# A Griffin-style decoder block on one core: the recurrence by decay products on VectorE, the output gate moved to the first block, and the sums of a wide block taken together

## The chip, the core and the metric

The kernel runs on one core of a Trainium2 chip. A core has TensorE (matrix multiply, results in PSUM banks of 128 x 512 float32), VectorE, ScalarE and GpSimd (elementwise work), and SyncE, which here only issues DMA. Every engine takes its instructions in order and waits on semaphores. The metric is the device time of one execution in microseconds (us). Times of before: 1763.41, 1767.73 and 1767.49, median 1767.49.

## What is computed

One layer of a decoder block on x of 256 x 2048, all float32 (the reference, shortened):

```python
a = rmsnorm(h, norm_mix_pre)
proj = a @ w_in                       # 2048 x 17408
q_a, k_a, v_a, q_r, f_r, i_r, g_r, gate_a, gate_r = split_columns(proj)
attn = ...   # 3 groups of 8 heads, windows 128, 512, 2048 with strides 1, 4, 16, rotary
q_h = silu(q_r); f = lb + (1 - lb) * sigmoid(f_r)         # 8 heads, 128 keys, 128 values
r_out = hgrn2(q_h, log(f), 1 - f, i_r)    # S_t = diag(f_t) S_{t-1} + k_t v_t^T, o_t = S_t^T q_t
r_out = rmsnorm_per_head(r_out) * gain * silu(g_r)        # g_r: the output gate
y = sigmoid(gate_a) * (attn @ w_attn_branch) + sigmoid(gate_r) * (r_out @ w_hgrn_branch)
h = h + rmsnorm(y @ w_mix_out, norm_mix_post)
gt, up = split(rmsnorm(h, norm_ffn_pre) @ w_ffn_gate_up)  # 2 x 5632 columns
h = h + rmsnorm((silu(gt) * up) @ w_ffn_down, norm_ffn_post)
```

The recurrence over 256 positions can be written as o_t = sum over s <= t of (q_t . D(s,t) k_s) v_s, with D(s,t) the product of the decays f after s up to t, for each of 128 keys. So per head it is a 256 x 256 lower triangle of weights, times v.

## The kernel before

**Weights.** All weights come as float32 through three buffers `raw` on SyncE's queue. A split makes two parts for TensorE: ScalarE copies `raw` into a rounded high part (`w`, L294 or L340), VectorE subtracts to get the low part (L295, or `wl` in L342). A product is three matmuls: high x high, high x low, low x high (`prod`, L372). The activations are split the same way (`Split`, L459; `transpose_in`, L509, makes `xT` with a ScalarE copy in L524 and a VectorE subtraction in L528).

**Items.** The program is one list of items, written out by hand in the loop at L1444. For item i it issues the split of item i+2 (`AHEAD`), the loads as far as the `raw` buffers reach, the matmuls of item i, then one turn of the evacuations (`evacs`), and one turn of each of two *lanes*. A lane is a queue of Python generators (the recurrence of half the heads, the attention of one head); each turn issues a generator's instructions up to its next `yield`. So on every engine the lanes' instructions stand between those of the weights.

**Wide blocks.** The first eight blocks (`early`, L1379) and the FFN work on 1024 columns in eight steps of 256 rows (`Wide`, `split_wide` L331, `multiply_wide` L363). Plain steps take 24 matmuls. In three steps of each block but the first, seven products of sums replace eight (21 matmuls): `split_wide` builds sums of weight quarters on VectorE (L346 to L353) and splits them in two sets, `w`/`wl` (L358 the last of it) and `dh`/`dl` (L360, VectorE's last instruction of such a split). The products p1, p5, p6 and p7 have banks of their own; after the third such step (`last7`) `gather` (L417) copies p1 on ScalarE (L421) and adds the others on VectorE (L422 to L425) into four tiles `b.rest`. The four banks of the block are added to them at its end, in `totals` (L705, sums in L712) for the early blocks and in `evac_ffn` (L1249, L1252) for the FFN. `totals` takes bank after bank: add, then use; a `yield` after every second one.

In these steps `by_sums` goes first and `by_raw`, which ends p1, second (L411). Between the two, and between the halves of a plain step, `between` gives the block's `mid` and the lanes a turn.

The first block has no seven-product steps. It is also where x is transposed: its `mid` (`more_x`, L663) transposes the next two row blocks of x in the middle of step c. The split of item c+2 and its loads stand before that in the program (L1454).

The order of the early blocks is: two of attention gates, one of the recurrence's branch gate, three of values v (these six go through a sigmoid or copy on ScalarE, L726, and to DRAM on ScalarE's queue, L729), then the output gate `g` (`evac_g`, L741: a sigmoid on ScalarE, L747, and two VectorE operations, L748 and L751, per bank), then the recurrence's values `i`.

**Chunks.** The projections for f, q of the recurrence and q, k of the attention come transposed, in steps of 16 matmuls (`multiply_chunk`). Their evacuations include the rotary embedding on VectorE (L786 to L793).

**The recurrence** (`recurrence`, L853) runs twice, for four heads each, on tiles of 128 keys x 1024 (head, position). VectorE clamps f at 2^-63, ScalarE takes Ln, VectorE scans it into running sums b (L870). Then blocks of size w = 1, 2, 4, ..., 32 are joined level by level: GpSimd subtracts the sum at the middle of each pair of blocks (L878), ScalarE takes Exp of both halves (L881, L882), VectorE multiplies the left half by k (L884), GpSimd the right half by q (L885), TensorE takes eight small products, and VectorE puts them into the weights `at` where a mask says so (L896). Levels 64 and 128 (`level64`, `level128`) and the diagonal (`same`) are alike. The levels depend on b alone, so a new one starts every second turn and several are under way at once.

Of the kernel before, what the change touches and what calls it, by code (L numbers as in the profile page):

```python
# [31 lines left out]
F_MIN = 2.0 ** -63  # L32
# [49 lines left out]
def tile_hybrid_block(ctx: ExitStack, tc: tile.TileContext, t, out):  # L82
# [13 lines left out]
    def nm(s):  # L96
        serial[0] += 1
        return f"{s}_{serial[0]}"
# [7 lines left out]
    def aux():  # L106
        return auxp.tile([P, 512], F32, tag="aux", name=nm("aux"))
# [60 lines left out]
    reset = kp.tile([P, 1024], F32, name="reset")  # L168
    nc.gpsimd.memset(reset, 1.0)
    nc.gpsimd.memset(reset.rearrange("p (n w) -> p n w", w=64)[:, :, 0:1], 0.0)  # L170
# [10 lines left out]
    def fslot(s):  # L181
        return fp[0].tile([P, 1024], F32, tag="f", bufs=16, name=nm(s))
# [90 lines left out]

    def multiply(i):
        kind, n = items[i][:2]
        if kind is chunks:
            multiply_chunk(n)
            return
        b, c = steps[n][:2]

        def between():
            if b.mid:
                b.mid(c)
            advance_lanes()

        multiply_wide(n, between=between)
# [76 lines left out]
    def multiply_wide(n, sides=(0, 1), groups=(0, 1), between=lambda: None):  # L363
# [341 lines left out]
    def totals(b, then):  # L705

        while "r1c" not in ready:
            yield
        for n, key in enumerate(((0, 0), (0, 1), (1, 0), (1, 1))):
            src = b.bank[key]  # L710
            if b.rest:
                nc.vector.tensor_add(b.rest[key], src, b.rest[key])  # L712
                src = b.rest[key]
            then(key, src)
            if n % 2:
                yield
# [136 lines left out]
    def recurrence(half):  # L853
# [4 lines left out]
        def spans(x, w):  # L858
            return x.rearrange("p (n w) -> p n w", w=w)

        kk, b, at = fslot("kk"), fslot("b"), fslot("at")
# [8 lines left out]
        nc.vector.tensor_tensor_scan(  # L870
            out=b, data0=reset, data1=f, initial=0.0, op0=OP.mult, op1=OP.add,
        )
        yield
        def level(lev, w):
            x = fslot("x")
            xv, bv, kv, qv = (spans(a, 2 * w) for a in (x, b, kk, q))
            n = 1024 // (2 * w)
            nc.gpsimd.tensor_sub(xv, bv, bv[:, :, w - 1 : w].to_broadcast([P, n, 2 * w]))  # L878
            yield
            left, right = slice(0, w), slice(w, 2 * w)  # L880
            nc.scalar.activation(xv[:, :, left], xv[:, :, left], AF.Exp, scale=-1.0)  # L881
            nc.scalar.activation(xv[:, :, right], xv[:, :, right], AF.Exp)  # L882
            yield
            nc.vector.tensor_mul(xv[:, :, left], xv[:, :, left], kv[:, :, left])  # L884
            nc.gpsimd.tensor_mul(xv[:, :, right], xv[:, :, right], qv[:, :, right])  # L885
            yield
            yield
            ps = aux()
            for e in range(8):
                xe = x[:, e * P : (e + 1) * P]  # L890
                mm(
                    spans(ps[:, e * 64 : (e + 1) * 64], w), xe,
                    spans(xe, 2 * w)[:, :, right], True, True,
                )
            yield
            nc.vector.copy_predicated(  # L896
                at.rearrange("p (e n w) -> p e n w", e=8, w=2 * w)[:, :, :, right],
                lmask[:, lev, :].rearrange("p (n w) -> p n w", w=w)[:, None, :, :]
                .to_broadcast([P, 8, 64 // w, w]).bitcast(I32),
                ps.rearrange("p (e n w) -> p e n w", e=8, w=w),  # L900
            )

        def level64():

            x = fslot("x")
            xe, be, ke, qe = (
                a.rearrange("p (e c t) -> p e c t", e=8, c=2) for a in (x, b, kk, q)
            )
            nc.gpsimd.tensor_sub(
                xe[:, :, 0, :], be[:, :, 0, :], be[:, :, 0, 63:64].to_broadcast([P, 8, 64])  # L910
            )
            yield
            nc.scalar.activation(xe[:, :, 0, :], xe[:, :, 0, :], AF.Exp, scale=-1.0)
            nc.scalar.activation(xe[:, :, 1, :], be[:, :, 1, :], AF.Exp)
            yield
            nc.vector.tensor_mul(xe[:, :, 0, :], xe[:, :, 0, :], ke[:, :, 0, :])
            nc.gpsimd.tensor_mul(xe[:, :, 1, :], xe[:, :, 1, :], qe[:, :, 1, :])
            yield
            yield
            ps = aux()  # L920
            for e in range(8):
                mm(ps[:64, e * 64 : (e + 1) * 64], xe[:, e, 0, :], xe[:, e, 1, :], True, True)
            yield
            nc.scalar.activation(
                at.rearrange("p (e t) -> p e t", e=8)[:64, :, 64:],
                ps[:64].rearrange("p (e t) -> p e t", e=8), AF.Copy,
            )

        def level128():

            x = fslot("x")
            xc, bc = (a.rearrange("p (h c t) -> p h c t", h=4, c=4) for a in (x, b))
            end = small("end")
            nc.vector.tensor_add(end[:, :4], bc[:, :, 0, 63], bc[:, :, 1, 63])
            nc.vector.tensor_sub(
                xc[:, :, 0, :], bc[:, :, 0, :], end[:, :4, None].to_broadcast([P, 4, 64])
            )
            nc.gpsimd.tensor_sub(
                xc[:, :, 1, :], bc[:, :, 1, :], bc[:, :, 1, 63:64].to_broadcast([P, 4, 64])
            )  # L940
            nc.gpsimd.tensor_add(
                xc[:, :, 3, :], bc[:, :, 3, :], bc[:, :, 2, 63:64].to_broadcast([P, 4, 64])
            )
            yield
            xh, kh, qh = (a.rearrange("p (h t) -> p h t", h=4) for a in (x, kk, q))
            nc.scalar.activation(xh[:, :, :P], xh[:, :, :P], AF.Exp, scale=-1.0)
            nc.scalar.activation(xc[:, :, 2, :], bc[:, :, 2, :], AF.Exp)
            nc.scalar.activation(xc[:, :, 3, :], xc[:, :, 3, :], AF.Exp)
            yield
            nc.vector.tensor_mul(xh[:, :, :P], xh[:, :, :P], kh[:, :, :P])  # L950
            nc.gpsimd.tensor_mul(xh[:, :, P:], xh[:, :, P:], qh[:, :, P:])
            yield
            yield
            ps = aux()
            for h in range(4):
                mm(ps[:, h * P : (h + 1) * P], xh[:, h, :P], xh[:, h, P:], True, True)
            yield
            a2.append(ptile("a2"))
            nc.scalar.activation(a2[0], ps, AF.Copy)

        def same():

            x = fslot("x")
            nc.gpsimd.tensor_mul(x, q, kk)
            yield
            yield
            ps = aux()
            for e in range(8):
                mm(ps[:, e : e + 1], x[:, e * P : (e + 1) * P], ones[:, 0:1], True, True)
            yield  # L970
            nc.vector.copy_predicated(
                at.rearrange("p (e t) -> p e t", e=8),
                ident[:, None, :].to_broadcast([P, 8, P]).bitcast(I32),
                ps[:, :8, None].to_broadcast([P, 8, P]),
            )

        a2 = []
        todo = [level(lev, w) for lev, w in enumerate(LEVELS)] + [same(), level64(), level128()]
        running, turn = [], 0
        while todo or running:  # L980
            if turn % 2 == 0 and todo:
                running.append(todo.pop(0))
            for r in list(running):
                try:
                    next(r)
                except StopIteration:
                    running.remove(r)
            turn += 1
            yield
        a2 = a2[0]  # L990
# [384 lines left out]
    def begin_wides():  # L1375
# [3 lines left out]
    early = [  # L1379
        (("a", 0), ("a", 1), COL_GA, 512),  # L1380
# [4 lines left out]
    early += [("g", "g", COL_GR, 512), ("i", "i", COL_IR, 512)]  # L1385
# [58 lines left out]
    for i in range(len(items)):  # L1444
# [94 lines left out]
```

## Time and profile before

| | us |
|---|---|
| times of three runs | 1763.41, 1767.73, 1767.49 |
| the profiled execution: time | 1764.46 |
| the profiled execution: span from the first to the last instruction | 1762.7 |
| mean granted TensorE clock over the span | 0.994 |

A row of the profile's groups or time line names the line of the kernel, engine, operation, output <- inputs by the program's names (buffer numbers left out), the shapes, and how many. In a time line start and duration stand in front, and in brackets how long the engine was idle before it and which instruction ended that. In a list of waits the numbers are us in total, times, and the longest. A row of busy times by stretch has the stretch, its length, then busy us of PE (TensorE's matmuls), PEld (its weight loads), DVE (VectorE), ACT (ScalarE) and POOL (GpSimd), each with the number of instructions, then the granted TensorE clock, the share of DMA time and GB/s. Matmuls overlap each other, so a matmul's drawn duration is longer than the distance to the next.

### The profile page before, as it was taken

How to read it: one execution, taken by the hardware profiler on the slowest of the kernel's cores; microseconds unless marked ns; L12 is line 12 of the kernel's file. 1: busy time of each engine (PE TensorE's matmuls, PEld its weight loads, DVE VectorE, ACT ScalarE, POOL GpSimd, SP SyncE). 2: the span in 40 equal slices, each digit the busy share in tenths (PEclk: the TensorE clock that was granted, in tenths of full speed). 3: DMA queues.
4: the chain of work that ended last, by engine and by line, in shares of the span. 5: the costliest groups of instructions: out<-in, count | busy, mean ns of one | idle time of the engine just before them, and what ended most of it. 6: DMA issues, size and time to landing. Idle time of an engine off the chain costs nothing.

```text
span 1762.7 us, 21573 instructions
## 1 busy us (share of the span) xinstructions
PE 1719.0 (98%) x8356; PEld 1432.1 (81%) x8357; DVE 1390.0 (79%) x1466; ACT 917.3 (52%) x1052; POOL 77.2 (4%) x54
## 2 busy tenths in 40 slices
PE   8999999899999999999999999999999999999997
PEld 6777777688888888888888877888888888788886
DVE  5878888866798997775566477888888888899998
ACT  6555555444534544445444466555555555565663
POOL 0000000000151241000000000000000000000000
PEclk9999999999999999999999999999999999999999
DMA  7656666465535534466555755555555555666563
GB/s 266 225 200 223 223 221 221 152 203 186 185 120 167 201 122 158 154 203 236 170 160 175 264 166 192 200 198 197 192 191 191 191 191 191 215 215 210 189 200 118
DMA packets 207190, 338.49 MB, mean 192 GB/s; under 512 B 10688, under 2 KB 77424, under 8 KB 207088
## 3 DMA queue, kind: packets, MB, share of 16 engines
q1 hardware_dynamic: 201360, 325.71, 55.8%
q10 hardware_dynamic: 5728, 11.41, 1.7%
q8 instruction: 65, 1.06, 0.3%
q14 instruction: 37, 0.30, 0.1%
HBM read 328.69 MB, written 8.39 MB: 191 GB/s over the span
## 4 chain that ended last, share of the span: by engine, by line
PE 70%; DVE 16%; issue 6%; ACT 5%; DMA 2%; ACTq 0%; POOL 0%; SPq 0%; DVEq 0%; POOLq 0%
PE acc L119 47%; PE aux L119 21%; DMA raw<-in_w_in 2%; DVE wl L358 2%; DVE wl L342 2%; DVE dl L360 2%; DVE w L295 2%; ACT w L354 1%; DVE e L1252 1%; DVE sum L346 1%; ACT w L340 1%; DVE sum L353 1%; DVE sum L352 1%; ACT e L726 1%; DVE e L1258 1%
## 5 line engine op out<-in xcount | busy, mean ns | idle before, releaser
L295 DVE TENSOR_TENSOR w<-raw,w 128x1024 fp32r<-128x1024 f32 x224 | 284.9, 1274 | 173.7 <-ACT w L294 172.8
L119 PE MATMUL acc<-xT,w 128*128 128x256 f32 (+1 forms) x2048 | 369.6, 340 | 5.2 <-DVE w L295 5.2
L294 ACT ACTIVATE w<-raw 128x1024 fp32r<-128x1024 f32 x224 | 236.3, 1057 | 255.6 <-PE acc L119 236.9
L119 PEld LDWEIGHTS acc<-xT,w 128*128 128x128 f32 x2048 | 312.4, 189 | 51.3 <-DVE w L295 7.4
L342 DVE TENSOR_TENSOR wl<-raw,w 128x2048 fp32r<-128x2048 f32 (+1 forms) x131 | 283.9, 2173 | 64.5 <-ACT w L340 61.6
L340 ACT ACTIVATE w<-raw 128x2048 fp32r<-128x2048 f32 (+1 forms) x131 | 237.3, 1817 | 71.0 <-issue 22.3
L358 DVE TENSOR_TENSOR wl<-sum,w 128x2048 fp32r<-128x2048 f32 x63 | 144.4, 2291 | 59.0 <-ACT w L354 57.7
L119 PE MATMUL acc<-w,hT 128*128 128x512 f32 x622 | 184.8, 391 | 1.5 <-DVE w L295 1.2
L119 PE MATMUL acc<-w,xT 128*128 128x512 f32 x578 | 172.4, 396 | 5.7 <-ACT xT L524 3.8
L351 ACT ACTIVATE w<-sum 128x1024 fp32r<-128x1024 f32 x63 | 66.9, 1062 | 171.1 <-DVE sum L346 168.3
L119 PE MATMUL aux<-w,hT 128*128 128x512 f32 x430 | 138.0, 389 | 0.0
L119 PEld LDWEIGHTS acc<-w,hT 128*128 128x128 f32 x622 | 115.8, 188 | 27.0 <-DVE w L295 2.5
L119 PEld LDWEIGHTS acc<-w,xT 128*128 128x128 f32 x578 | 108.8, 190 | 29.7 <-ACT xT L524 4.2
L119 PE MATMUL aux<-w,xT 128*128 128x512 f32 x344 | 112.3, 395 | 1.6 <-ACT w L340 1.6
L360 DVE TENSOR_TENSOR dl<-raw,dh 128x1536 fp32r<-128x1536 f32 x63 | 110.3, 1752 | 0.0
L357 ACT ACTIVATE dh<-raw 128x1536 fp32r<-128x1536 f32 x63 | 93.2, 1480 | 4.7 <-PE aux L119 2.1
L119 PEld LDWEIGHTS aux<-w,hT 128*128 128x128 f32 x430 | 80.7, 188 | 16.7
L119 PE MATMUL acc<-w,yT 128*128 128x512 f32 x384 | 88.2, 390 | 0.0
L119 PE MATMUL acc<-w,a 128*128 128x512 f32 x268 | 83.8, 389 | 1.7 <-DVE e L1252 1.7
L119 PEld LDWEIGHTS acc<-w,yT 128*128 128x128 f32 x384 | 71.8, 188 | 15.2 <-DVE w L295 0.4
L119 PE MATMUL aux<-w,a 128*128 128x512 f32 x268 | 83.7, 389 | 0.0
L119 PE MATMUL aux<-wl,hT 128*128 128x512 f32 x215 | 83.6, 389 | 0.0
(278 smaller groups left out, 2742.9 us busy)
## 6 DMA issues: line engine op xcount, KB each, us to landing
raw<-in_w_in SPq DMA_DIRECT2D x270, 512.0 KB, 4.6
raw<-in_w_ffn_gate_up SPq DMA_DIRECT2D x176, 512.0 KB, 4.6
raw<-in_w_ffn_down SPq DMA_DIRECT2D x88, 512.0 KB, 4.8
raw<-in_w_mix_out SPq DMA_DIRECT2D x32, 512.0 KB, 4.9
raw<-in_w_hgrn_branch SPq DMA_DIRECT2D x16, 512.0 KB, 4.9
raw<-in_w_attn_branch SPq DMA_DIRECT2D x16, 512.0 KB, 4.7
waits<-e ACTq DMA_DIRECT2D x24, 256.0 KB, 4.6
v<-waits SPq DMA_DIRECT2D x6, 512.0 KB, 8.2
```

What stands on the lines that cost most here:

```text
L119: nc.tensor.matmul(ps, lhsT, rhs, start=start, stop=stop, skip_group_check=True)
L294: nc.scalar.activation(wh, raw, AF.Copy)
L295: nc.vector.tensor_sub(wl, raw, wh.bitcast(F32))
L340: nc.scalar.activation(hi[:, c], raw[:, c], AF.Copy)
L342: nc.vector.tensor_sub(lo[:, c], raw[:, c], hi[:, c].bitcast(F32))
L346: nc.vector.tensor_sub(s[:, :1024].rearrange("p (a c) -> p a c", a=2), raw[:, 512:1536].rearrange("p (a c) -> p a c", a=2), raw[:, None, : ...
L351: nc.scalar.activation(hi[:, :1024], s[:, :1024], AF.Copy)
L352: nc.vector.tensor_add(s[:, 1024:1536], raw[:, 512:1024], s[:, 512:1024])
L353: nc.vector.tensor_sub(s[:, 1536:], raw[:, 1536:], s[:, 1024:1536])
L357: nc.scalar.activation(dhi, d, AF.Copy)
L358: nc.vector.tensor_sub(lo, s, hi.bitcast(F32))
L360: nc.vector.tensor_sub(dlo, d, dhi.bitcast(F32))
```

## The change

Five edits, the diff cut to its core.

1. The first block is the output gate `g`; the others keep their order.
2. Where a wide block has a `mid` (only the first block), the split of item i+2 and its loads are issued in the middle of step i, behind the transposes, and no longer ahead of the step.
3. In the third seven-product step of a block (where the activations need no preparation) `by_raw` goes first, so that p1 is complete 12 matmuls before the step's end.
4. `totals` adds all four banks to `b.rest` in one go, and uses them in the next two turns.
5. The recurrence. No Ln, no scan, no Exp. k and q are kept multiplied by the decay products of their block, in place: after the products of a level are taken, the left halves of k are multiplied by the whole product of the right block, and the right halves of q by that of the left block; the block products (`end`) are multiplied in pairs. All of it is on VectorE; only the clearing of `at` stays on GpSimd. One level follows the other: products, one turn later the mask copy and three multiplies, two turns later the next products. The float32 pool gets 17 tiles instead of 16, in place of the tile `reset`.

```diff
@@ prepare, multiply
+    def prepare(i):
+        split(i + AHEAD)
+        if i + AHEAD < len(items):
+            load_upto(items[i + AHEAD][2] + N_RAW)
...
         def between():
             if b.mid:
                 b.mid(c)
+                prepare(i)
             advance_lanes()
@@ multiply_wide
-        for part in (by_raw, by_sums) if b.prep else (by_sums, by_raw):
-            part()
-            if part is by_raw or not b.prep:
-                between()
-                between = lambda: None
+        first, second = (by_raw, by_sums) if b.prep or last else (by_sums, by_raw)
+        first()
+        between()
+        second()
@@ totals
-        for n, key in enumerate(((0, 0), (0, 1), (1, 0), (1, 1))):
-            src = b.bank[key]
-            if b.rest:
-                nc.vector.tensor_add(b.rest[key], src, b.rest[key])
-                src = b.rest[key]
-            then(key, src)
-            if n % 2:
+        keys = ((0, 0), (0, 1), (1, 0), (1, 1))
+        if b.rest:
+            for key in keys:
+                nc.vector.tensor_add(b.rest[key], b.bank[key], b.rest[key])
+            yield
+        for key in keys:
+            then(key, b.rest[key] if b.rest else b.bank[key])
+            if key == (0, 1):
                 yield
@@ recurrence
-        nc.vector.tensor_scalar(f, f, F_MIN, None, op0=OP.max)
-        yield
-        nc.scalar.activation(f, f, AF.Ln)
-        yield
-        nc.vector.tensor_tensor_scan(
-            out=b, data0=reset, data1=f, initial=0.0, op0=OP.mult, op1=OP.add,
...
+        nc.vector.tensor_mul(x, q, kk)
+        yield
+        nc.vector.tensor_mul(q, q, f)
+        yield
+        ps = aux()
+        for e in range(8):
+            mm(ps[:, e : e + 1], x[:, e * P : (e + 1) * P], ones[:, 0:1], True, True)
+        yield
+        nc.vector.copy_predicated(
...
+        ends, used, end = fslot("end"), 0, f
+        for lev, w in enumerate(LEVELS):
             ps = aux()
             for e in range(8):
+                es = slice(e * P, (e + 1) * P)
                 mm(
+                    spans(ps[:, e * 64 : (e + 1) * 64], w), kk[:, es],
+                    spans(q[:, es], 2 * w)[:, :, w:], True, True,
                 )
             yield
             nc.vector.copy_predicated(
...
+            n = 1024 // (2 * w)
+            end = spans(end, 2)
+            for x, l, r in ((kk, slice(0, w), 1), (q, slice(w, 2 * w), 0)):
+                y = spans(x, 2 * w)[:, :, l]
+                nc.vector.tensor_mul(y, y, end[:, :, r : r + 1].to_broadcast([P, n, w]))
+            new = ends[:, used : used + n]
+            used += n
+            nc.vector.tensor_mul(new, end[:, :, 0], end[:, :, 1])
+            end = new
+            yield
+            yield
...
+        end = spans(end, 2)
+        for x, c in ((ke, 0), (qe, 1)):
+            nc.vector.tensor_mul(
+                x[:, :, c, :], x[:, :, c, :],
+                end[:, :, 1 - c : 2 - c].to_broadcast([P, 8, 64]),
+            )
...
@@ the early blocks and the loop
     early = [
+        ("g", "g", COL_GR, 512),
         (("a", 0), ("a", 1), COL_GA, 512),
...
-    early += [("g", "g", COL_GR, 512), ("i", "i", COL_IR, 512)]
+    early += [("i", "i", COL_IR, 512)]
...
-        split(i + AHEAD)
-        if i + AHEAD < len(items):
-            load_upto(items[i + AHEAD][2] + N_RAW)
+        if not (wide and b.mid):
+            prepare(i)
```

More of the change, by code (lines that the diff above doesn't have):

```diff
@@ L961, in same @@
[L961 to L990, printed above, removed]
+        qe, ke = (x.rearrange("p (e c t) -> p e c t", e=8, c=2) for x in (q, kk))
@@ L991, in recurrence @@
+        yield
+        yield
+        ps = aux()
+        qh, kh = (x.rearrange("p (h t) -> p h t", h=4) for x in (q, kk))
+        for h in range(4):
+            mm(ps[:, h * P : (h + 1) * P], kh[:, h, :P], qh[:, h, P:], True, True)
+        yield
+        a2 = ptile("a2")
+        nc.scalar.activation(a2, ps, AF.Copy)
+        yield
         v = iN[half]
```

86 lines of the change are left out of this document (12 added, 74 removed).

## The prediction, made before the change was run

> **What bounds the kernel now.** I read the page's head first, then the list of what TensorE waits for (us in total, times, longest), then the busy times by stretch.
>
> ```profile
> span 1762.7 us, 21573 instructions
> PE 1719.0 (98%) x8356; PEld 1432.1 (81%) x8357; DVE 1390.0 (79%) x1466; ACT 917.3 (52%) x1052; POOL 77.2 (4%) x54
> ```
>
> ```profile
> PE acc L119 <- DVE w L295: 6.4, 6, 2.0
> PE acc L119 <- ACT xT L524: 3.8, 1, 3.8
> PE aux L119 <- DVE wl L342: 3.6, 3, 1.8
> ...
> PE acc L119 <- DVE wl L342: 2.5, 3, 1.0
> ...
> PE aux L119 <- DVE x L884: 2.1, 2, 1.1
> PE acc L119 <- DVE xT L528: 1.8, 2, 1.1
> ```
>
> ```profile
> 6.79:60.00 53.21, 47.54 (x210) 37.78 (x208) 36.87 (x63) 32.05 (x55) 0.00 (x0) 0.94 0.71 249
> 108.00:325.00 217.00, 211.41 (x920) 171.73 (x920) 177.94 (x141) 115.16 (x94) 0.00 (x0) 1.00 0.66 219
> 325.00:350.00 25.00, 19.48 (x71) 14.55 (x70) 19.82 (x20) 12.47 (x11) 0.00 (x0) 0.86 0.29 103
> 475.00:545.00 70.00, 66.65 (x409) 58.52 (x408) 69.36 (x63) 30.18 (x44) 34.16 (x18) 0.98 0.44 141
> 600.00:670.00 70.00, 65.93 (x419) 58.16 (x418) 67.33 (x66) 30.64 (x46) 32.82 (x17) 1.00 0.49 165
> 690.00:760.00 70.00, 70.00 (x428) 61.99 (x427) 50.23 (x84) 33.32 (x64) 0.00 (x0) 1.00 0.47 153
> 1130.00:1500.00 370.00, 365.08 (x1631) 299.32 (x1630) 316.12 (x258) 197.19 (x164) 0.00 (x0) 1.00 0.57 191
> ```
>
> TensorE is the bound: busy for 1719.0 of 1762.7. The change takes no matmul away and adds none (each level of the recurrence keeps its products), so all that can move is TensorE's lost time: 43.7 us idle, and what runs at a lowered clock (the column after POOL's). The waits name weights and activations that VectorE or ScalarE had not finished, no transfers. The stretches show five places: the first block; the ends of the wide blocks (108 to 325); the output gate's block end (325 to 350); the two recurrences (475 to 545 and 600 to 670, where VectorE is full and GpSimd works); and the FFN blocks (1130 to 1500). From 690 to 760, with the same matmuls and no GpSimd, nothing is lost.
>
> **Part 1: in the first block the transposes go ahead of the next split.**
>
> ```profile
> 20.73 1.06 ACT L340 ACTIVATE w<-raw 128x1024 fp32r<-128x1024 f32 x1 [0.23 <-DMA raw<-in_w_in]
> 21.69 0.82 ACT L524 ACTIVATE xT<-aux,colg 128x256 fp32r<-128x256 f32 x2
> ```
>
> ```profile
> 22.20 0.79 PE L119 MATMUL acc<-w,xT 128*128 128x512 f32 x1 [3.78 <-ACT xT L524]
> ...
> 24.94 1.05 PE L119 MATMUL acc<-w,xT 128*128 128x512 f32 x2
> 25.79 0.63 PE L119 MATMUL acc<-wl,xT 128*128 128x512 f32 x1
> ```
>
> ScalarE, in order, stood at a split whose weights were still in flight; the activation copies queued behind it (21.69), and TensorE waited 3.78. In the new order the copies come first, and the step that they feed has its own weights already. The split that is now later belongs to the step after, so the 3.78 goes; what is late next is that split, needed one step (24 matmuls, 5.5 us) later. The two waits for L528 (1.8) have the same cause. Idle in the stretch is 53.21 - 47.54 = 5.67. After the long wait the matmuls run at half rate: two in 25.79 - 24.94 = 0.85, against 211.41 / 920 = 0.23 each in the second stretch; a clock of 0.94 over 53.21 is 3.2 more. Together 8.9. VectorE then also has the sums for the seven-product steps, so I leave 0.9 and take **8.0** (ends 6 and 9). The weight loads that move with the split wait for its buffer, as now; behind them SyncE holds only block 0's small loads, the norm gain among them.
>
> The Trainium skill ("TensorE: Matmul & The Clock Gate", "Why this matters for your kernels") says that the clock drops after idle gaps above about 3 us. By that rule only this place would lose clock. Yet the stretch from 325 shows 0.86 while its longest wait is 1.8. By the rule moving the gate would gain no clock, 2.6 less (8.8 below, minus 5.52 idle and four stalls), and the time be 1731.
>
> **Part 2: block ends.** VectorE's, then ScalarE's, then TensorE's rows at one of them:
>
> ```profile
> 157.40 1.28 DVE L712 TENSOR_TENSOR e<-acc,e 128x512 f32<-128x512 f32 x2
> 162.38 2.29 DVE L342 TENSOR_TENSOR wl<-raw,w 128x2048 fp32r<-128x2048 f32 x1 [3.70 <-ACT w L340]
> ```
>
> ```profile
> 160.43 1.92 ACT L340 ACTIVATE w<-raw 128x2048 fp32r<-128x2048 f32 x1 [0.46 <-ACT e L726]
> ```
>
> ```profile
> 163.53 0.39 PE L119 MATMUL aux<-w,xT 128*128 128x512 f32 x1
> 164.73 0.50 PE L119 MATMUL aux<-wl,xT 128*128 128x512 f32 x1 [0.81 <-DVE wl L342]
> ```
>
> The second pair of sums (157.40) stands behind a whole split on VectorE; ScalarE's two activations wait for it, its copy of the next weights (160.43) for them, and VectorE idles 3.70 for that copy. TensorE loses 1.20 - 0.23 = 0.97, so 0.16 more than its idle figure; I add that per stall. With all four sums at the block's end ScalarE never waits for the second pair, and VectorE's gap should shrink to some 1.5 (two activations of ScalarE still lie ahead of its copy): 2.2 earlier, more than the 0.97 and the smaller stall behind it. The stretch loses 5.59 idle + 10 stalls x 0.16 = 7.2 over five ends. There will be six such ends; I leave 0.2 each.
>
> ```profile
> 339.35 0.75 DVE L748 SCALAR_TENSOR_TENSOR sig<-e,r1c,sig 128x512 f32<-128x512 f32 x1 [0.79 <-ACT sig L747]
> 340.13 0.69 DVE L751 TENSOR_TENSOR g<-sig,gainr 128x512 f32<-128x512 f32 x1
> ```
>
> The gate adds 4 x (0.75 + 0.69) = 5.8 on VectorE; its block stores nothing, so ScalarE's four store issues move from the first block's end to another, and the weight loads only change places. At 325 to 350 that comes on top of a seven-product block: 71 matmuls where 25 / 0.23 = 109 fit, 38 x 0.23 = 8.8 lost. As the first block it has no sums of its own, and VectorE is 36.87 / 53.21 = 69% busy there, against 177.94 / 217.00 = 82%. Its 5.8 still falls into block 1's first splits, cover of 0.18 x 43 = 7.8 free VectorE time a block. If that is gone it costs up to 5.8; I take 1.0. Part 2: 7.2 + 8.8 - 1.2 - 1.0 = **13.8** (9 to 16).
>
> **Part 3: the recurrence.** Groups of VectorE by form, first from 475 to 545, then the split from 690 to 790:
>
> ```profile
> L295 DVE TENSOR_TENSOR w<-raw,w 128x1024 fp32r<-128x1024 f32 x18 | 27.9, 1554 | 0.0
> L884 DVE TENSOR_TENSOR x<-x,kk 128x512 f32<-128x512 f32 x6 | 11.1, 1856 | 0.1
> ...
> L870 DVE TENSOR_TENSOR_SCAN b<-reset,f 128x1024 f32<-128x1024 f32 x1 | 2.3, 2282 | 0.0
> ...
> L916 DVE TENSOR_TENSOR x<-x,kk 128x512 f32<-128x512 f32 x1 | 0.7, 694 | 0.0
> L935 DVE TENSOR_TENSOR x<-b,end 128x256 f32<-128x256 f32 x1 | 0.4, 425 | 0.0
> L934 DVE TENSOR_TENSOR end<-b 128x4 f32<-128x4 f32 x1 | 0.2, 158 | 0.0
> ```
>
> ```profile
> L295 DVE TENSOR_TENSOR w<-raw,w 128x1024 fp32r<-128x1024 f32 x30 | 36.7, 1223 | 24.5 <-ACT w L294 24.1
> ```
>
> Beside GpSimd the same instructions take longer: 18 x (1.554 - 1.223) = 6.0 and 6 x (1.856 - 0.694) = 7.0, at least 13.0 us per half. Removed from VectorE per half: the scan 2.28, the clamp (some 0.7), eight multiplies 8 x 0.694 = 5.6, and 0.6 of level 128: 9.1. Added: two full multiplies 2 x 1.22, fourteen halves 14 x 0.694 = 9.7, and six products of block ends, 0.69 + 0.42 + 4 between 0.16 and 0.42: 14.1. VectorE: 69.36 + 5.0 - 13.0 = 61 of 70. ScalarE loses all 18 Ln and Exp; the GpSimd memset stays.
>
> The new wait: a level's products need the multiplies of the level before, and behind them TensorE holds the next weights' matmuls. A level takes three turns of 16 matmuls, 3 x 16 x 70 / 428 = 7.9 us; its four VectorE instructions are 4 x 0.69 = 2.8. At 690 to 760 VectorE is free for 28%, 2.2 of 7.9, and there with attention beside it. At worst 0.6 for each of 12 levels, 7; at best none. The first half has no attention, so I take 1.0. Lost today: 3.35 + 4.07 idle, 1.1 for some seven stalls, 0.02 x 70 = 1.4 of clock: 9.9. Part 3: **9.0** (3 to 10).
>
> Instructions on VectorE go from 20 per half (four to begin, 6 x 2, one, three) to 30 (four, 6 x 4, two). The Trainium skill ("VectorE: DVE Perf Modes", "Rules for kernel authors") asks for as few operations as possible, against this part. The shortest here takes 0.158; twenty more would be 3.2 for both halves and the time 1731, were they on the path; the durations above contain that share.
>
> **Part 4: p1 first in the last seven-product step.** One boundary of the FFN:
>
> ```profile
> 1124.16 0.69 DVE L422 TENSOR_TENSOR e<-acc,e 128x512 f32<-128x512 f32 x1 [1.10 <-ACT e L421]
> ```
>
> ```profile
> 1140.03 0.33 PE L1218 MATMUL aux<-ident,e 128*128 128x128 f32 x1 [0.21 <-DVE e L1258]
> 1140.69 0.98 PE L1218 MATMUL aux<-ident,e 128*128 128x128 f32 x7 [0.33 <-DVE e L1258]
> ```
>
> VectorE waits 1.10 for ScalarE's copy of p1, today the last product; everything behind it, to the inputs of the transposes, is as late. With p1 ready 12 matmuls earlier (2.7) the 1.10 goes, more than the 0.54 idle here. Nine ends: 4.92 idle + 18 x 0.16 = 7.8. I take **7.5** (4 to 9).
>
> Sum: 8.0 + 13.8 + 9.0 + 7.5 = 38.3. The profiled execution took 1764.46 (its span 1762.7 and 1.8 around it), so 1726.2. It lay 3.0 under the median of the runs, 1767.49; I put the new median halfway, at 1728.
>
> **Rivals.** *VectorE stays full in the recurrence*: for it speaks the count 20 to 30, against it the 13.0. Part 3 is nothing: 1737.
>
> *The last split part is late*: p1 needs `dl`, which VectorE writes last.
>
> ```profile
> 180.47 1.75 DVE L360 TENSOR_TENSOR dl<-raw,dh 128x1536 fp32r<-128x1536 f32 x1
> ```
>
> ```profile
> 180.84 0.39 PE L119 MATMUL acc<-w,so 128*128 128x512 f32 x1
> ```
>
> Today that step starts 1.4 before `dl` is done. Without the 2.2 of part 2, seven early blocks lose 1.2 each: 8.4, so 1736.
>
> *The gate's stall only moves* to the end of block 0: 7.8 more, 1736.
>
> *Slower: the levels are a chain.* Today several are under way at once. If each of 16 levels put its 2.8 fully on the path, that is 45, and 1764.5 - 29.3 - 9.9 + 45 = 1770, plus the clock. It decides from 39 / 16 = 2.5 per level. Against it: two turns lie between the multiplies and the next products.
>
> *Nothing changes*: TensorE gives the time back elsewhere, by a lower clock; 690 to 760 at 1.00 speaks against it.
>
> **How the numbers follow.** Forecast 0.64, VectorE full 0.12, late `dl` 0.09, gate moved 0.07, chain 0.05, nothing 0.03. The forecast's own ends (6 + 9 + 3 + 4 = 22 to 44) give 1720 to 1745; the range 1717 to 1746 takes in the three smaller gains. About 0.3%, 5 us, can be told from no change: faster 0.92, same 0.03, slower 0.05.
>
> **What would show it.** No wait for `xT` at 20 us, clock 1.00 there; no DVE gap near 3.7 at block ends; the matmuls of 325 to 350 without a hole; GpSimd empty and VectorE under 90% at 475 to 545, the split back at 1.22; transposes without a wait. I am wrong if waits for `kk` or `q`, or for `dl`, stand in TensorE's list with over 5 us.

## The result and the profile after

After: 1724.36 us, median of four runs (1724.13 to 1725.07). Before, in four runs: 1767.51 (1763.41 to 1767.73). The ratio is 0.9762, with a 95% interval of 0.9745 to 0.9779. The profiled execution of after took 1724.25, its span 1722.5. Over this study the runs of before spread from 1761.80 to 1768.75, the longest at a mean granted clock of 0.991 and the shortest at 0.996, so a difference of a few us to before says little by itself.

The head of the page of after, then what TensorE waits for (us in total, times, longest):

```profile
span 1722.5 us, 21496 instructions
...
PE 1704.8 (99%) x8357; PEld 1430.4 (83%) x8357; DVE 1359.9 (79%) x1486; ACT 899.0 (52%) x1016; POOL 6.5 (0%) x16
```

```profile
PE acc L118 <- DVE wl L360: 1.8, 1, 1.8
PE acc L118 <- DVE w L297: 1.4, 3, 0.7
...
PE acc L118 <- DVE sig L750: 0.9, 1, 0.9
...
PE aux L118 <- DVE dl L362: 0.7, 1, 0.7
```

TensorE's idle time went from 43.7 to 1722.5 - 1704.8 = 17.7. The waits for `xT`, for the chunks' splits and for `wl` L342 (now L344) are gone or small. Three are left that belong together, `wl` L360, `sig` L750 and `dl` L362: all lie between 67 and 93 us, at the end of the first block. Busy times of after by stretch; each stretch is moved with the work, so that it answers to one of before:

```profile
6.79:60.00 53.21, 52.66 (x243) 42.15 (x242) 40.16 (x71) 33.38 (x59) 0.00 (x0) 1.00 0.77 269
60.00:75.00 15.00, 12.27 (x46) 9.20 (x45) 13.13 (x14) 7.54 (x8) 0.00 (x0) 0.90 0.32 112
100.00:310.00 210.00, 210.00 (x928) 173.91 (x927) 180.67 (x143) 116.54 (x96) 0.00 (x0) 1.00 0.67 230
...
460.00:530.00 70.00, 70.00 (x447) 62.34 (x446) 57.19 (x78) 25.44 (x32) 0.00 (x0) 1.00 0.47 152
...
1090.00:1465.00 375.00, 375.00 (x1693) 311.40 (x1692) 326.19 (x268) 203.97 (x170) 0.00 (x0) 1.00 0.59 200
```

Where before lost time in five places, four now lose nothing or nearly nothing. The new hole is from 60 to 75: 46 matmuls where 15 / 0.227 = 66 fit (0.227 is 10.88 / 48, from the chain below), so 20 x 0.227 = 4.5 us, and a clock of 0.90.

The chain of work that ended last gives the stages' bounds, first of before, then of after (start, length, TensorE's line, matmuls):

```profile
371.77 100.33 PE acc L119 x576
...
899.31 19.06 PE acc L119 x84
...
1520.93 22.05 PE acc L119 x96
```

```profile
103.94 10.88 PE acc L118 x48
...
145.42 10.88 PE aux L118 x48
...
352.82 103.10 PE acc L118 x592
...
869.05 19.06 PE acc L118 x84
...
1480.73 22.05 PE acc L118 x96
```

Chunks begin 18.95 earlier, the branches 30.26, the down projection 40.20. Two blocks of seven products lie 41.48 apart. From 103.94 to 352.82 are six times 41.48: there nothing stalls any more. Seven blocks without a stall would take 290.4, so that 296.8 for blocks 1 to 7 is 6.4 lost, all of it ahead of 103.94.

The table has the length of each stage in every profile of this study, from TensorE's first matmul in it to the first of the next (all other stages stay within 0.5 us), and the times. The kernels ran in several sessions on different chips, each beside runs of before of its own, to which the ratio goes; the stage lengths are those of one profiled execution each. Blocks are counted from 0.

| kernel | to block 1 | blocks 1 to 7 | chunks | FFN | median | ratio to before (95%) |
|---|---|---|---|---|---|---|
| before | 63.4 | 308.4 | 527.3 | 483.8 | 1767.51 | |
| after | 56.1 | 296.8 | 515.9 | 473.6 | 1724.36 | 0.9762 (0.9745 to 0.9779) |
| split first | 64.5 | 293.6 | 515.9 | 473.7 | 1728.62 | 0.9793 (0.9776 to 0.9809) |
| gate seventh | 57.2 | 295.9 | 515.9 | 473.6 | 1723.38 | 0.9762 (0.9743 to 0.9782) |
| sums in pairs | 56.7 | 308.0 | 516.0 | 473.7 | 1735.46 | 0.9832 (0.9815 to 0.9848) |
| p1 last | 56.6 | 296.9 | 515.9 | 483.8 | 1733.60 | 0.9823 (0.9806 to 0.9840) |
| old recurrence | 55.9 | 296.8 | 532.8 | 473.6 | 1740.07 | 0.9860 (0.9844 to 0.9877) |
| recurrence alone | 63.6 | 306.5 | 516.0 | 483.7 | 1751.81 | 0.9930 (0.9915 to 0.9945) |
| sums alone | 62.5 | 295.4 | 529.3 | 484.1 | 1753.44 | 0.9935 (0.9921 to 0.9948) |
| GpSimd beside | 55.9 | 296.8 | 532.6 | 473.6 | 1741.17 | 0.9870 (0.9856 to 0.9885) |
| GpSimd tied | 57.9 | 296.7 | 532.1 | 473.6 | 1742.67 | 0.9868 (0.9854 to 0.9882) |
| bounds late | 56.2 | 296.5 | 516.0 | 473.7 | 1724.09 | 0.9774 (0.9759 to 0.9788) |
| bounds early | 58.7 | 299.2 | 515.9 | 473.7 | 1730.13 | 0.9797 (0.9783 to 0.9812) |
| bounds early, gain late | 58.8 | 298.1 | 515.9 | 473.6 | 1728.82 | 0.9790 (0.9775 to 0.9804) |

The four gains of after are 7.3, 11.6, 11.4 and 10.2. Each experiment moves one column or two by more than 2 us, so a difference can be laid at its place.

### The profile page after: what moved, and what is told of

Its sections match the earlier page's. It is cut to its first block, busy times and chain, and to the rows that moved or that the text cites. A ratio compares the mean times of both kernels' runs of the same rounds, so it can differ in the third digit from the quotient of the medians.

```text
span 1722.5 us, 21496 instructions
## 1 busy us (share of the span) xinstructions
PE 1704.8 (99%) x8357; PEld 1430.4 (83%) x8357; DVE 1359.9 (79%) x1486; ACT 899.0 (52%) x1016; POOL 6.5 (0%) x16
## 4 chain that ended last, share of the span: by engine, by line
PE 91%; DVE 4%; ACT 2%; DMA 2%; issue 1%; SPq 0%; DVEq 0%; ACTq 0%
PE acc L118 60%; PE aux L118 29%; DMA raw<-in_w_in 1%; DVE wl L344 1%; ACT w L342 0%; PE aux L834 0%; DMA gpost<-in_norm_mix_post 0%; PE aux L1160 0%; DVE fz L1289 0%; DVE wl L360 0%; DVE w L297 0%; DVE dl L362 0%; PE acc L1160 0%; DMA x<-in_x 0%; PE aux L518 0%
## 5 line engine op out<-in xcount | busy, mean ns | idle before, releaser
L297 DVE TENSOR_TENSOR w<-raw,w 128x1024 fp32r<-128x1024 f32 x224 | 274.0, 1224 | 193.1 <-ACT w L296 191.3
L344 DVE TENSOR_TENSOR wl<-raw,w 128x2048 fp32r<-128x2048 f32 (+1 forms) x131 | 284.3, 2173 | 51.1 <-ACT w L342 49.4
L342 ACT ACTIVATE w<-raw 128x2048 fp32r<-128x2048 f32 (+1 forms) x131 | 237.9, 1820 | 103.7 <-PE acc L118 38.2
L360 DVE TENSOR_TENSOR wl<-sum,w 128x2048 fp32r<-128x2048 f32 x63 | 144.3, 2291 | 57.4 <-ACT w L356 57.4
L362 DVE TENSOR_TENSOR dl<-raw,dh 128x1536 fp32r<-128x1536 f32 x63 | 110.4, 1752 | 0.0
L118 PEld LDWEIGHTS aux<-w,hT 128*128 128x128 f32 x430 | 80.7, 188 | 16.8
```

The costliest lines, as they stand in the source:

```text
L118: nc.tensor.matmul(ps, lhsT, rhs, start=start, stop=stop, skip_group_check=True)
L297: nc.vector.tensor_sub(wl, raw, wh.bitcast(F32))
L342: nc.scalar.activation(hi[:, c], raw[:, c], AF.Copy)
L344: nc.vector.tensor_sub(lo[:, c], raw[:, c], hi[:, c].bitcast(F32))
L360: nc.vector.tensor_sub(lo, s, hi.bitcast(F32))
L362: nc.vector.tensor_sub(dlo, d, dhi.bitcast(F32))
```

## The experiments

The theory was the prediction's: four gains that add up, each from its own mechanism. The rivals were that some parts give nothing, or that the gain of one is another's.

### The first block's split ahead of the transposes again

```diff
             if b.mid:
                 b.mid(c)
-                prepare(i)
...
-        if not (wide and b.mid):
-            prepare(i)
+        prepare(i)
```

> The changed kernel with one edit undone: in the first block the split of item i+2 and its loads stand ahead of the step again. If ScalarE's copies of the transposed x really hang behind a split whose weights are in flight, TensorE's wait for xT of some 3.8 us comes back at about 20 us with the half clock behind it, block 1 starts 7 us later (63 for 56), and the time is 1731 to 1732. Rival: the first block is short of VectorE or of transfers, and the place of the split only moves the wait: block 1 starts within 3 us of 56, time under 1727.5.

Measured: 1728.62, 4.3 over after, between the ranges of the theory and of the rival. The wait of before is back, with the half rate behind it:

```profile
22.84 0.79 PE L118 MATMUL acc<-w,xT 128*128 128x512 f32 x1 [3.83 <-ACT xT L524]
...
25.58 1.05 PE L118 MATMUL acc<-w,xT 128*128 128x512 f32 x2
```

Block 1 starts 8.4 later, but blocks 1 to 7 are 3.2 shorter. The stretch that answers to 60 to 75 lies 8.4 later here, and the hole in it is small:

```profile
68.40:83.40 15.00, 14.57 (x63) 11.44 (x62) 13.67 (x14) 7.38 (x7) 0.00 (x0) 1.00 0.38 127
```

So the reordering does what was predicted, and over a third of it is given back one block later. A likely reading is that VectorE and ScalarE run ahead while TensorE waits, and the gate then falls into that lead; it was not tried by itself.

### The gate back in seventh place

```diff
     early = [
-        ("g", "g", COL_GR, 512),
...
-    early += [("i", "i", COL_IR, 512)]
+    early += [("g", "g", COL_GR, 512), ("i", "i", COL_IR, 512)]
```

> The changed kernel with the output gate back in seventh place among the early blocks; all else as changed. By the prediction the gate's 5.8 us of VectorE work is the dearer on top of a seven-product block: its block end loses 6 to 9 us there, the first block's end loses nothing, and since the end of block 0 loses 5.9 now, the time is 1724 to 1728. Rival: with the four sums taken together the gate's end costs no more than its VectorE work beyond the block's slack, 2 or less, and the move itself costs: 1718 to 1721.

Measured: 1723.38 (1723.05 to 1724.38), as after, and in neither range. The hole is back where before had it, and the one behind the first block is gone:

```profile
60.00:75.00 15.00, 15.00 (x68) 12.31 (x67) 11.13 (x12) 9.66 (x10) 0.00 (x0) 1.00 0.70 249
...
325.00:350.00 25.00, 22.28 (x97) 17.75 (x97) 22.40 (x20) 13.21 (x11) 1.86 (x2) 1.00 0.57 190
```

Here 25 / 0.227 = 110 matmuls fit, 97 are there: 13 x 0.227 = 3.0 lost, against 8.8 in before and the 6 to 9 of the theory. Over blocks 1 to 7 it loses 295.9 - 290.4 = 5.5, after 6.4. The move itself is worth nothing: the gate's work costs 3 to 5 at either place, and most of the hole of before did not come from the gate's place.

### The sums of a wide block in pairs, and together alone

The first kernel is after with the loop of before in `totals`; the second is before with the loop of after. For the first:

```diff
-        keys = ((0, 0), (0, 1), (1, 0), (1, 1))
-        if b.rest:
-            for key in keys:
-                nc.vector.tensor_add(b.rest[key], b.bank[key], b.rest[key])
-            yield
...
+            if b.rest:
+                nc.vector.tensor_add(b.rest[key], src, b.rest[key])
+                src = b.rest[key]
```

> The changed kernel with totals as before: add, use, add, use, yield. If the sums taken together are what freed the block ends, six ends lose 1.4 us each again and VectorE's gap of 3.7 us is back: 1731 to 1733. Rival: it was p1 going first (VectorE starts its gather 1 us earlier and stays ahead), and the ends lose at most 0.4 each: under 1727.

> The kernel before, with nothing of the change but the four sums of a wide block together. Theory (that alone is the gain of the early seven-product blocks): 11 to 12 under the kernel before, 1751 to 1753, blocks 1 to 7 taking 297 to 298 us. Rival (it takes the gate's move too): 4 to 8 under, 1755.5 to 1759.5, the hole at 325 to 350 still there.

Measured: undone, 1735.46, 11.1 over after and 2.5 over the theory's range, with blocks 1 to 7 at 308.0 as in before. Alone, 1753.44, and these blocks at 295.4; the time is 0.4 over the theory's range, and the chunks, which this edit leaves as they were, take 2.0 longer than in before. The busy times of the first kernel at the block ends and VectorE at one of them, then the busy times of the second at the gate (the gate in seventh place):

```profile
100.00:310.00 210.00, 205.01 (x893) 166.36 (x891) 171.73 (x137) 113.29 (x94) 0.00 (x0) 1.00 0.64 218
```

```profile
161.33 2.29 DVE L344 TENSOR_TENSOR wl<-raw,w 128x2048 fp32r<-128x2048 f32 x1 [3.69 <-ACT w L342]
```

```profile
325.00:350.00 25.00, 22.40 (x91) 17.78 (x90) 22.55 (x18) 12.12 (x10) 0.00 (x0) 0.93 0.50 165
```

Blocks 1 to 7 lose 17.6 over the 290.4 without this edit in after, 18.0 in before, and 5.0 with this edit alone: it is the whole gain of the early blocks. It also fills part of the gate's hole, 91 matmuls against 71 before, where the gate's own sums came in pairs too; 19 of 110 are still missing, 4.3 us. At a block end of after VectorE looks like this:

```profile
144.83 2.48 DVE L713 TENSOR_TENSOR e<-acc,e 128x512 f32<-128x512 f32 x4
...
156.53 2.29 DVE L344 TENSOR_TENSOR wl<-raw,w 128x2048 fp32r<-128x2048 f32 x1 [1.55 <-ACT w L342]
```

All four sums stand ahead of the split, and VectorE's idle time for ScalarE's copy is 1.55, where it was 3.70 in before and is 3.69 with the sums in pairs.

### p1 last again

```diff
-        first, second = (by_raw, by_sums) if b.prep or last else (by_sums, by_raw)
+        first, second = (by_raw, by_sums) if b.prep else (by_sums, by_raw)
```

> The changed kernel with by_sums first in the last seven-product step, as before. If the wait of VectorE for the copy of p1 makes the transposes of the FFN late, 0.9 us at nine block ends and about 1 at the last come back: 1732.5 to 1734, all of it in the FFN, and the early blocks lose under 1. Rival: the FFN's ends were freed by something else that is still there: under 1727.

Measured: 1733.60, 9.2 over after, as the theory had it, all of it in the FFN, which is at before's 483.8. The transposes wait again, in 18 places for 4.9 in all as in before; in after's list these waits are gone. One of the two rows:

```profile
PE aux L1160 <- DVE e L1200: 2.7, 10, 0.3
```

The early blocks don't feel it (296.9): their block ends need no transposes of `e`.

### The old recurrence in after, and the new one in before

Both exchange the body of `recurrence` with that of the other kernel, and the tile `reset` with the seventeenth slot.

> The changed kernel with the recurrence of before (Ln, scan, Exp, GpSimd) and all other edits kept. If the recurrence's stretch lost about 10 us to itself alone, the stages add up: 1734 to 1736, with VectorE full and its splits at 1.55 us in that stretch. Rival: the stages lean on each other (a kernel that arrives with more lead absorbs the old recurrence): under 1730.

> The kernel before with the new recurrence alone. By the same theory 10 to 11.5 us less than the kernel before, ratio 0.9935 to 0.9945, and only the stretch of the chunks gets shorter. Rival: part of the gain there comes from the other edits: less than 8 us.

Measured: 1740.07, 15.7 over after and 4 over the theory's range, and 1751.81, 11.5 under the runs of before beside it (1763.29), at the upper end of what was expected. In the first only the chunk stage differs, 532.8; in the second it is at 516.0, and blocks 1 to 7, which the edit does not touch, are 1.9 shorter than in before as well. The granted clock from 325 to 350 was 0.93 there and 0.86 in before.

The first loses 5.5 more in the chunk stage than before did with the same recurrence. TensorE's idle time is no longer, 532.80 - 525.95 = 6.85 against 527.30 - 519.88 = 7.42; the clock is lower. All four runs of this kernel have a mean clock of 0.992 to 0.994 over the span; why it is lower here is not shown. Without these 5.5 the old recurrence costs the 11.4 by which the stage got shorter from before to after. The chunk stage of before, then of the kernel with the old recurrence:

```profile
371.80:899.10 527.30, 519.88 (x3057) 454.26 (x3055) 390.69 (x488) 253.27 (x381) 70.61 (x37) 1.00 0.53 172
```

```profile
352.60:885.40 532.80, 525.95 (x3056) 459.61 (x3055) 390.81 (x486) 253.57 (x381) 71.53 (x38) 0.98 0.52 169
```

Busy times of the kernel with the old recurrence, and two of its VectorE groups from 455 to 525; then the same groups' counterparts in after from 460 to 530:

```profile
455.00:525.00 70.00, 66.65 (x401) 58.49 (x400) 68.22 (x63) 28.70 (x40) 33.87 (x17) 0.95 0.42 135
```

```profile
L301 DVE TENSOR_TENSOR w<-raw,w 128x1024 fp32r<-128x1024 f32 x18 | 27.9, 1553 | 2.7 <-ACT w L300 2.7
L890 DVE TENSOR_TENSOR x<-x,kk 128x512 f32<-128x512 f32 x6 | 11.1, 1854 | 0.1
```

```profile
L297 DVE TENSOR_TENSOR w<-raw,w 128x1024 fp32r<-128x1024 f32 x21 | 25.7, 1225 | 12.3 <-ACT w L296 11.8
...
L901 DVE TENSOR_TENSOR kk<-kk,end 128x512 f32<-128x512 f32 x5 | 3.4, 687 | 0.0
```

More instructions and less time: 78 in 57.19 us against 63 in 68.22. Beside GpSimd the 18 splits and 6 multiplies took 5.9 and 7.0 us longer than at the means of after, which is more than the whole difference.

### Work on GpSimd beside the new recurrence

Two kernels ask whether it was GpSimd. Each adds two subtractions of 128x1024 on GpSimd to a level; nobody reads their results. In the first nothing holds them back, in the second a small ScalarE copy of the level's block ends does:

```diff
             end = new
+            flag = small("flag")
+            nc.scalar.activation(flag, new[:, :8], AF.Copy)
             yield
+            for _ in range(2):
+                nc.gpsimd.tensor_sub(spare, lone, flag[:, 0:1].to_broadcast([P, 1024]))
             yield
```

> The changed kernel; beside each level of the new recurrence GpSimd does two subtractions of 128 x 1024 on two tiles that nobody else uses, 12 per half, some 31 us of GpSimd time per half as in the kernel before. Nothing waits for them. If GpSimd's being busy is what made VectorE slow, the splits beside it rise from 1.22 to about 1.5 us, VectorE fills up and TensorE loses again: with the longer VectorE list of the new recurrence 5 to 20 us, 1729 to 1744. Rival: it was the handing over between GpSimd, ScalarE and VectorE in each level, not GpSimd's traffic: within 1.5 us of the changed kernel.

> The changed kernel, with two subtractions of 128x1024 on GpSimd in each level of the recurrence, whose results nobody uses; a small ScalarE copy of the level's block ends holds them back, so that they run beside the recurrence (some 28 us a half against 34 in the kernel before). Theory (GpSimd slows VectorE there, and that is what the old recurrence cost): VectorE's splits there go from 1.22 to 1.4 or more and the multiplies by block ends from 0.69 to 1 or more, VectorE over 90% at 455 to 525; 8 to 18 slower, 1732 to 1742. Rival (the old recurrence's cost was its own chain of exponentials and its order): under 1727, VectorE under 85%.

Measured: 1741.17 and 1742.67, 16.8 and 18.3 over after. In the first the work did not run where it was meant to. GpSimd takes its instructions in order and had nothing to wait for, so it ran them at 350 to 440, before the recurrence had begun; there the time was lost, and the recurrence's own stretch stayed full, so that the two tiles that the work takes cost it nothing:

```profile
350.00:440.00 90.00, 79.87 (x420) 66.86 (x419) 70.80 (x56) 34.22 (x47) 63.74 (x27) 0.94 0.47 152
455.00:525.00 70.00, 70.00 (x437) 62.43 (x436) 56.92 (x74) 26.79 (x33) 0.00 (x0) 1.00 0.51 166
```

VectorE's groups from 350 to 440 in this kernel, and then in after:

```profile
L297 DVE TENSOR_TENSOR w<-raw,w 128x1024 fp32r<-128x1024 f32 x25 | 42.0, 1702 | 17.7 <-ACT w L296 17.7
L686 DVE TENSOR_SCALAR f<-f,lb,lb 128x256 f32<-128x256 f32 x8 | 15.1, 1922 | 0.0
...
L216 DVE TENSOR_TENSOR sum<-acc,sum 128x256 f32<-128x256 f32 x12 | 4.4, 409 | 0.0
```

```profile
L297 DVE TENSOR_TENSOR w<-raw,w 128x1024 fp32r<-128x1024 f32 x31 | 37.9, 1224 | 34.2 <-ACT w L296 34.2
L216 DVE TENSOR_TENSOR sum<-acc,sum 128x256 f32<-128x256 f32 x14 | 5.2, 416 | 0.0
L686 DVE TENSOR_SCALAR f<-f,lb,lb 128x256 f32<-128x256 f32 x8 | 2.9, 408 | 0.0
```

TensorE, which is busy for all of this stretch in after, is idle for 10.1 of the 90 us here: 7.9 for splits and 2.2 for ScalarE's copies. The chunk stage takes 532.6, 16.7 more than in after. So GpSimd's work alone, without any of the old chain of exponentials, lengthens VectorE's work beside it and can cost TensorE as much as the new recurrence had gained, though here at another place and in one dense run, 63.74 us in 90. A full VectorE isn't needed for that: it is busy for 70.80 of 90.

The second kernel puts the work where it was meant to be:

```profile
455.00:525.00 70.00, 66.41 (x405) 57.93 (x404) 61.93 (x67) 21.16 (x33) 23.24 (x10) 0.98 0.42 136
```

```profile
L297 DVE TENSOR_TENSOR w<-raw,w 128x1024 fp32r<-128x1024 f32 x18 | 30.7, 1718 | 7.7 <-ACT w L296 7.6
```

TensorE loses 3.6 in this stretch, as with the old recurrence (3.35), and in its list of waits the splits stand with 9.4 us. But this kernel also has a wait that the first one and the old recurrence do not have. The small copy waits for the last multiply of its level, and ScalarE's copies of the weights queue behind it. ScalarE's wait from 440 to 700, then ScalarE and VectorE at one level:

```profile
ACT flag L913 <- DVE end L910: 84.0, 12, 9.0
```

```profile
504.46 0.21 ACT L913 ACTIVATE flag<-end 128x8 f32<-128x8 f32 x1 [8.97 <-DVE end L910]
504.58 1.04 ACT L296 ACTIVATE w<-raw 128x1024 fp32r<-128x1024 f32 x1
```

```profile
505.65 2.14 DVE L297 TENSOR_TENSOR w<-raw,w 128x1024 fp32r<-128x1024 f32 x1 [1.22 <-ACT w L296]
```

The chain of work that ended last goes through that copy in five levels running, from 481 to 528 us. How much of the 18.3 comes from it and how much from splits of 1.72 stays open, so the answer rests on the first kernel. Two details of the expectation fell as well: VectorE is at 61.93 of 70, not over 90%, and the multiplies kept their 0.69 (L907, a mean of 693 ns), since they had no GpSimd work beside them.

### The end of the first block: the lower bounds late, early, and the gain spread

Of the 6.4 that after loses in blocks 1 to 7, the expectations put 5.9 at the end of the first block. ScalarE and VectorE there:

```profile
58.52 1.28 ACT L749 ACT_TABLE_LOAD   x1
59.82 1.27 ACT L749 ACTIVATE sig<-acc,r1c 128x512 f32<-128x512 f32 x2
```

```profile
60.54 0.75 DVE L750 SCALAR_TENSOR_TENSOR sig<-acc,r1c,sig 128x512 f32<-128x512 f32 x1 [1.19 <-ACT sig L749]
...
63.33 1.22 DVE L348 TENSOR_TENSOR sum<-raw 128x1024 f32<-128x1024 f32 x1
...
67.12 2.29 DVE L360 TENSOR_TENSOR wl<-sum,w 128x2048 fp32r<-128x2048 f32 x1 [1.13 <-ACT w L356]
```

Ahead of the gate's sigmoids come the Exp of the recurrence's lower bounds, and block 1's first sums (63.33) come behind half of the gate. Three kernels move these: the bounds 16 turns later; their load, transpose and Exp into the first turns; and this with the four multiplies by the gain one to a turn. The first of them:

```diff
         nc.vector.tensor_copy(colg[:, 16:48], ps[:, :32])
+        for _ in range(16):
+            yield
```

> The changed kernel with the lower bounds' small operations (nine of VectorE, two Exp and a table load of ScalarE) 16 lane turns later, out of the end of block 0. If these, and not the gate's own 5.8 us, make the first split of block 1 late (it starts 7 us after the block does), most of the 5.9 us lost there goes: 1719 to 1721. Rival: the gate's eight operations alone are too much: 1723 to 1725.

> The changed kernel, but the lower bounds are loaded and worked out in the first turns of block 0 and not at its end. Theory (TensorE's wait at the end of block 0, 5.9 us in all, comes mostly from ScalarE: the bounds' two Exp and a table load stand ahead of the gate's sigmoids): the waits at 63 to 73 us fall to 3 or less and nothing comes back in block 2, 1719 to 1722. Rival (it is the gate's 5.8 us on VectorE that TensorE waits for): no change, 1723.5 to 1726.

> As the run before, and the four multiplies by the gain (0.69 us each) are put one to a turn behind the gate's other work. Theory (a lump of VectorE work costs TensorE, the same work spread costs less): 1717 to 1720, no wait over 1 us at 60 to 75. Rival (VectorE has no time to spare in the seven-product blocks, so 2.8 us cost the same wherever they fall): as the run before within 1 us.

Measured: 1724.09, 1730.13 and 1728.82: none beats after. The first lies in its rival's range; the second lies outside both of its ranges, and so does the third, at 1.3 under the second. Late bounds fill most of the hole and open others in block 2 (rows of the kernel with late bounds):

```profile
60.00:75.00 15.00, 14.19 (x61) 11.11 (x60) 13.70 (x13) 6.96 (x7) 0.00 (x0) 1.00 0.39 131
100.00:310.00 210.00, 208.24 (x916) 171.44 (x916) 179.20 (x148) 117.31 (x98) 0.00 (x0) 1.00 0.67 231
```

With early bounds the sigmoids start at 56.42, and the time is lost twice over for other reasons. In its list of waits:

```profile
PE aux L118 <- DVE colg L638: 6.4, 1, 6.4
PE acc L118 <- ACT xT L528: 1.9, 1, 1.9
```

The first is a PSUM bank: the transposed gain now comes a little later, its copy out of the bank (L638) stands on VectorE behind half the gate and a whole split, and block 1's next products need that bank. The second follows the bounds' small work in its new place, seven instructions of 0.16 to 0.20 on VectorE at 38.56 to 40.11. So the two early kernels decide nothing about the old wait: they measure two new ones. That spreading the gain's multiplies gains 1.3 beside them says little more. What part of the 5.9 is the gate's work on VectorE and what the wait for ScalarE stays open; that it does not pay to take the gate away from there follows from the gate in seventh place.

## Why the prediction was right, and where it was not

The total was right: 1724.36 in a range of 1717 to 1746, 3.6 under the 1728. The profiled execution was to take 1726.2 and took 1724.25. The median of after lies at its profiled execution, so that half of the 3.0, added for the median, was not needed.

That the total is so close is in part luck: parts 3 and 4 gained 5.1 more than forecast, each beyond its own upper end, and parts 1 and 2 gained 2.9 less.

- **Part 1, 8.0:** 7.3 by the start of block 1, the wait and the half rate gone as described. By the experiment it is worth 4.3 net, since blocks 1 to 7 take 3.2 longer with it; the reason given above is likely and was not tried.
- **Part 2, 13.8:** 11.6, near it by luck. The step that failed is the gate's: "At 325 to 350 that comes on top of a seven-product block" put all of the 8.8 lost there down to the gate's place, and "I take 1.0" was to be left of it. The move gains nothing (1723.38 against 1724.36): in the old place, with the sums together, the gate loses 3.0. The block ends, put at 7.2 less 1.2, are worth 11.1, as undoing them shows: the sums in pairs made most of the gate's hole as well. The prediction split one stretch between two edits of which one had caused most of it. The rival "the gate's stall only moves" had the mechanism right, with 6.4 in place of its 7.8, but its total of 1736 wrong, for it too put only 6 on the sums.
- **Part 3, 9.0 (3 to 10):** 11.4 in the chunk stage, 11.5 by time as the only edit, 15.7 when undone in after, where the clock was lower and the stage 5.5 longer than in before. The mechanism was right: splits at 1.22, multiplies at 0.69, no wait for `kk` or `q` in the list of waits. VectorE was put at 61 of 70 and is at 57.19. Two terms were mis-sized. The 1.0 taken for the levels' new wait is not there. And all 7.42 of the stage's idle time lay in the two stretches that were read, but beside it the stage lost 4.0, where the prediction had 1.1 for stalls and 1.4 for the clock.
- **Part 4, 7.5 (4 to 9):** 10.2, or 9.2 when undone. Again the mechanism was right. The stretch that was read (1130 to 1500) leaves out the last end, where TensorE's idle time went from 1.6 (1500 to 1520.9) to 0.4 (1470 to 1480.7 in after); the nine others give 1.0 each, where 7.8 had put 0.87.
- **Rivals:** VectorE is not full (57.19 of 70); the levels are no chain for TensorE. `dl` is late once, for 0.7, not seven times; with the sums in pairs it is late six times, 6.3 in all, so that rival was right about what happens "without the 2.2 of part 2".

Undone one by one, the edits cost 4.3 + 11.1 + 9.2 + 15.7 - 1.0 = 39.3; after is 43.1 faster by the medians and 40.2 by the spans. So they nearly add up, and what is left over is within the 7 us over which the runs of before are spread.

## What to carry to other kernels

Before putting a stall down to one of two edits, ask which of them makes it go alone: a hole behind a heavy step can be the fault of the sums around it. Take a stage's loss as its length less its length without a stall, from its first to its last instruction: idle time leaves out what comes behind a wait, and a convenient window leaves out an end. Look for new waits in a kernel that was made to test a cause: the copy that held GpSimd's work back held the weights back too. And count the instructions of VectorE only after asking what runs on GpSimd beside them: ten more per half took less time here, with GpSimd empty.

## What was not expected of the hardware

Which VectorE instructions GpSimd slows depends on where their operands lie. From 350 to 440, beside its subtractions, the split went from 1.224 to 1.702 and a multiply-add of 128x256 from 0.408 to 1.922 (L686), whereas sums of the same size that read a PSUM bank stayed at 0.41 (L216). The Trainium skill ("SBUF — State Buffer", "SBUF: two separate sides") says that GpSimd and VectorE share a pair of ports, held for a whole instruction by the one that came first, and that this concerns VectorE instructions with two inputs from SBUF, beside a GpSimd operation that reads SBUF, or in a mode that uses both ports. The rows agree: GpSimd's subtractions took 1.90 to 2.96 each in that kernel, so an instruction of 0.41 that has to wait for one is lengthened by a multiple, and one with a PSUM input not at all. Which of the two kinds the multiply-add is, no run here shows.

The clock also fell after short waits: 0.90 from 60 to 75 in after, where the longest wait is 1.8 (`wl` L360), as from 325 to 350 in before, 0.86 with a longest wait of 1.8 too. The rule of the Trainium skill that the prediction weighed ("TensorE: Matmul & The Clock Gate", "Why this matters for your kernels"), gaps above about 3 us, does not describe these two stretches.
